# A decoder layer on one core: z_b projected before z_a, and silu(z_a) kept in SBUF instead of sent through DRAM

## The chip, the cores and the metric

The kernel runs on one core of a Trainium2 chip. The metric is device time in microseconds for one execution: the median of the timed runs. Five engines work side by side, each through its own instruction list in order: TensorE (PE in the rows; PEld is its weight load), VectorE (DVE), ScalarE (ACT), GpSimd (POOL) and SyncE (SP), which here only issues transfers. ACT and POOL issue some transfers too.

## The reference: what is computed

One inference step of a hybrid decoder layer, for 1024 prompt positions and 64 sample positions with the same weights (all float32).

```python
h = x @ w_in + b_in        # split into a_val, a_gate, z_a (1024 wide), q, k, v, z_b (512), g_a, g_b (1024)
u = a_val * sigmoid(a_gate)
conv_raw = depthwise_conv(u, width 31)
attn = combination of three groups of dilated window attention over q, k, v
c  = silu(layer_norm(conv_raw + conv_b, conv_ln_g, conv_ln_b))
pa = (c * silu(z_a)) @ w_a
pb = (attn * silu(z_b)) @ w_b
m  = sigmoid(g_a) * pa + sigmoid(g_b) * pb
y  = layer_norm(ALPHA * x + m @ w_out, ln_g, ln_b)
```

The convolution's layer norm runs over the 1024 channels of a position. The key/value buffers and the last 30 rows of `u` are outputs too.

## The kernel before, in words

Activations lie with 128 channels on the partitions and the 1088 positions along the row. The positions are cut into three chunks (`CHUNKS`: 384, 352 and 352). A tile of a projection is 128 output channels by 1088 positions. For precision every operand of a projection is kept as a rounded part and a remainder (`hi` and `lo`, `xhi` and `xlo`, `hbh` and `hbl`, `hah` and `hal`); `split` makes them, the rounded part by a copy on ACT (L100), the remainder by a subtraction on DVE (L101). Each chunk is then a run of matmuls (L171) with three products for each 128 input channels: 24 matmuls for 1024 input channels, 12 for the 512 of w_b.

A chunk gathers in one of three PSUM banks (`mm`), from which ACT or DVE moves it out. Weight tiles come through two buffers each of `raw`, `hi` and `lo` (`load_w`). Everything else lies in numbered slots of a row each (`slot(i, ...)`), and in small half-row tiles: `sb`, `P` and `PT`, two buffers each.

The stages that matter here come at the end:

- After attention, `gate` projects a tile of g_b, g_a or z_a, applies sigmoid or silu on ACT on the way out of PSUM (`gst`, L730), and sends the row to DRAM (`sgb`, `sga`, `sza`, L732). The eight tiles of g_b and the eight of g_a are done by then.
- The layer norm of the convolution: the eight rows `cv` are read back from DRAM, their mean over channels is a sum on DVE (`chan_mean`) and a matmul with `ones` (L773); then the mean is subtracted (L777), squared on ACT and summed (L783), a second matmul with `ones` (L790) gives the variance, and each row is scaled (L803) and goes through silu (L804). Meanwhile PE projects four tiles of z_a.
- Then the four tiles of z_b, each followed by one more tile of z_a. A chunk of z_b goes through silu (ACT, L818), is multiplied by `attn` (DVE, L819) and split into `hbh` and `hbl`, by way of the half-row tile `sb`.
- Stage w_b: eight tiles with the weights `w_b`, 12 matmuls a chunk. Each chunk leaves PSUM by a multiplication with its piece of sigmoid(g_b) into `tf` (L839), the piece having been loaded from `sgb` into `P` or `PT` by SP (`ld`, L829). In the same stage silu(z_a) is loaded back from `sza` into `sb`, chunk by chunk, multiplied by `cv` on DVE (L848) and split into `hah` and `hal`, which take the memory of `xhi` and `xlo` (named `x` in the rows).
- Stage w_a: eight tiles with the weights `w_a` on `hah` and `hal`; then the projection w_out and the last layer norm.

The program order below is not the order on the engines: a scheduler places each engine's instructions by its own model, at build time. On the chip each engine keeps that order and waits where something is not ready.

Of the kernel before, what the change touches and what calls it, by code (L numbers as in the profile page):

```python
# [8 lines left out]
F32 = mybir.dt.float32  # L9
F32R = mybir.dt.float32r  # L10
AF = mybir.ActivationFunctionType
ALU = mybir.AluOpType
# [4 lines left out]
P = 128  # L17
# [4 lines left out]
NT = NP_ + NS  # L22
CHUNKS = ((0, 384), (384, 352), (736, 352))
# [4 lines left out]
F_AVAL, F_AGATE, F_ZA, F_Q, F_K, F_V, F_ZB, F_GA, F_GB = 0, 8, 16, 24, 36, 48, 60, 64, 72  # L28
# [13 lines left out]
def trunk_kernel(ctx, tc, I, O):  # L42
    nc = tc.nc
    sync, act, dve, pool, pe = nc.sync, nc.scalar, nc.vector, nc.gpsimd, nc.tensor
# [8 lines left out]
    dram = ctx.enter_context(tc.tile_pool(name="dram", bufs=1, space=DRAM))  # L53
# [3 lines left out]
    def nm(s):  # L57
        uid[0] += 1
        return f"{s}_{uid[0]}"

    def slot(i, shape, dt=F32, n="s"):
        return sp.tile(shape, dt, tag=f"S{i}", name=nm(n))

    def xslot(i, shape, dt=F32R, n="x"):
        return xs.tile(shape, dt, tag=f"X{i}", name=nm(n))

    def half(tag, shape, bufs, dt=F32):
        return hp.tile(shape, dt, tag=tag, bufs=bufs, name=nm(tag))
# [30 lines left out]
    def split(dst_hi, dst_lo, src):  # L99
        h = act.activation(out=dst_hi, in_=src, func=AF.Copy)  # L100
        dve.tensor_tensor(out=dst_lo, in0=src, in1=dst_hi.bitcast(F32), op=ALU.subtract)  # L101
        return h
# [7 lines left out]
    def load_w(src, n, raw=None, parts=1):  # L110
        if raw is None:
            raw = wp.tile([P, D], F32, tag="raw", name=nm("raw"))
            sync.dma_start(out=raw[:, :n], in_=src)
        hi = wp.tile([P, D], F32R, tag="hi", name=nm("hi"))
        lo = wp.tile([P, D], F32R, tag="lo", name=nm("lo"))
        with tc.high_priority(HP):
            for i in range(0, n, n // parts):
                s = split(hi[:, i:i + n // parts], lo[:, i:i + n // parts], raw[:, i:i + n // parts])
            pace(s)
        return hi, lo  # L120
# [53 lines left out]
    def proj(parts, evac):  # L174
        for ci, (c0, cn) in enumerate(CHUNKS):
            evac(ci, c0, cn, proj_chunk(parts, c0, cn))

    def in_proj(f, evac, w=None):
        hi, lo = w or load_w(I["w_in"][f], D)
        proj([(hi, lo, xhi, xlo)], evac)  # L180
# [28 lines left out]
    def rotate(key, slots):  # L209
        i = rot.get(key, 0)  # L210
        rot[key] = i + 1
        return slots[i % len(slots)]
# [89 lines left out]
    def visit(burst=None):  # L302

        with tc.high_priority(700):
            gate = pipe[-1]["exp"] if pipe else None
            if pipe and "pts" not in pipe[-1]:
                transposes(pipe[-1])
            if len(pipe) == 2 or burst is None:
                values(pipe.pop(0), gate)
            if burst:  # L310
                scores(burst, gate)
                pipe.append(burst)

    def together(m, gate):
        tc.add_manual_dep(m.ins, gate.ins.name, SYNC, reason="the row starts complete")
# [249 lines left out]
    for u, (f, g) in enumerate(units):  # L565
# [16 lines left out]
        if u in B_CONV:  # L582
            c = B_CONV.index(u)
# [137 lines left out]

    sga = dram.tile([8, P, NT], F32, name="sga")
    sgb = dram.tile([8, P, NT], F32, name="sgb")
    sza = dram.tile([8, P, NT], F32, name="sza")

    def gate(f, func, dst):
        st = slot(rotate("gst", GST), [P, NT], n="gst")

        def ev(ci, c0, cn, ps):
            act.activation(out=st[:, c0:c0 + cn], in_=ps, func=func, bias=b_sb[:, f:f + 1])  # L730
        in_proj(f, ev)
        pool.dma_start(out=dst, in_=st)  # L732

    GST = [3, 4]
    gates = ([(F_GB + i, AF.Sigmoid, sgb[i]) for i in range(8)] + [(F_GA + i, AF.Sigmoid, sga[i]) for i in range(8)]
             + [(F_ZA + i, AF.Silu, sza[i]) for i in range(8)])
    credit[1] = 0.0
    for pr in range(4):
        sc = sample_scores(pr)
# [10 lines left out]
            gate(*gates.pop(0))  # L750
    sample_out()
    credit[1] = 1.25
    GST[:] = [4, 5]
    cv = []
    for c in range(8):
        t = slot(6 + c, [P, NT], n="cv")
# [30 lines left out]
    for c0, cn in CHUNKS:  # L787
        ps = o_ps()
        s = slice(c0, c0 + cn)
# [14 lines left out]
        act.activation(out=cv[c], in_=cv[c], func=AF.Silu, scale=clg[:, c:c + 1], bias=clb[:, c:c + 1])  # L804


    hb_slots = (18, 19, 20, 21, 22, 23, 2, 3)
    hbh, hbl = [], []
    for _ in range(4):
        gate(*gates.pop(0))  # L810
    for f in range(4):
        hh = slot(hb_slots[2 * f], [P, NT], F32R, n="hbh")
        hl = slot(hb_slots[2 * f + 1], [P, NT], F32R, n="hbl")

        def ev(ci, c0, cn, ps, f=f, hh=hh, hl=hl):
            s = slice(c0, c0 + cn)
            z = half("sb", [P, 384], 2)
            act.activation(out=z[:, :cn], in_=ps, func=AF.Silu, bias=b_sb[:, F_ZB + f:F_ZB + f + 1])  # L818
            dve.tensor_tensor(out=z[:, :cn], in0=z[:, :cn], in1=attn[f][:, s], op=ALU.mult)  # L819
            split(hh[:, s], hl[:, s], z[:, :cn])  # L820
        in_proj(F_ZB + f, ev)
        hbh.append(hh)
        hbl.append(hl)
        gate(*gates.pop(0))


    def ld(tag, src, c0, cn):
        t = half(tag, [P, 384], 2)
        sync.dma_start(out=t[:, :cn], in_=src[:, c0:c0 + cn])  # L829
        return t[:, :cn]  # L830

    tf = []
    for i in range(8):
        hi, lo = load_w(I["w_b"][i], 512)
        t = slot((0, 1, 14, 15, 16, 17, 4, 5)[i], [P, NT], n="tf")
        sg = [ld(rotate("sg", ("P", "PT")), sgb[i], c0, cn) for c0, cn in CHUNKS]

        def ev(ci, c0, cn, ps, t=t, sg=sg):
            dve.tensor_tensor(out=t[:, c0:c0 + cn], in0=ps, in1=sg[ci], op=ALU.mult)  # L839
        proj([(hi, lo, hbh, hbl)], ev)  # L840
        tf.append(t)
    hah, hal = [], []
    for c in range(8):
        hh, hl = xslot(c, [P, NT]), xslot(8 + c, [P, NT])
        for c0, cn in CHUNKS:
            s = slice(c0, c0 + cn)
            z = ld("sb", sza[c], c0, cn)
            dve.tensor_tensor(out=z, in0=z, in1=cv[c][:, s], op=ALU.mult)  # L848
            split(hh[:, s], hl[:, s], z)
        hah.append(hh)  # L850
        hal.append(hl)
    for i in range(8):
# [7 lines left out]


    woh, wol = [], []
    wo_slots = (18, 19, 20, 21, 22, 23, 2, 3, 6, 7, 8, 9, 10, 11, 12, 13)
    for k in range(8):
        raw = wp.tile([P, D], F32, tag="raw", name=nm("raw"))
        sync.dma_start(out=raw, in_=I["w_out"][:, k])
# [9 lines left out]
    while copies:  # L876
        dst, src = copies.pop(0)
        act.dma_start(out=dst, in_=src)
    for t in range(9):
        n = min(P, NT - t * P)  # L880
# [8 lines left out]
        for hf in range(2):  # L889
            ps = mm_ps()  # L890
            s = slice(512 * hf, 512 * hf + 512)
# [14 lines left out]
        for hf in range(2):  # L906
            s = slice(512 * hf, 512 * hf + 512)
# [138 lines left out]
```

## Time and profile before

| what | value |
|---|---|
| median of three timed runs | 1432.5 us (1430.51 to 1432.59) |
| the profiled execution, its own time | 1428.53 us |
| its span, first to last instruction | 1426.7 us |
| PE busy | 1400.8 us, 98% of the span |
| DVE busy | 843.2 us, 59% |
| ACT busy | 448.6 us, 31% |
| mean granted TensorE clock | 0.996 of full speed |

The profiled execution took 1.8 us more than its span, and was 4.0 us shorter than the median. Busy shares are averages over all stages. "Idle before" or "waited for" is the time that an engine stood still before an instruction, with what ended that wait.

### The profile page before, as it was taken

Reading aid. Unit: us, or ns where it says so; the run is one execution under the profiler, and the core shown is the slowest. Engines: PE = TensorE matmul, PEld = TensorE weight load, DVE = VectorE, ACT = ScalarE, POOL = GpSimd, SP = SyncE. Lnnn points to the kernel's source line nnn. Section 1 sums busy time; section 2 is a strip of 40 time slices with the busy share of each in tenths; the row PEclk is TensorE's granted clock in tenths of the full one; section 3 lists DMA queues with packets and bytes.
Section 4 is the critical chain, followed back from the end, with each engine's and each line's share of the span. In section 5 each row is a group of like instructions: output and inputs, shape, how many; then the busy total and the mean of one; then the engine's idle time right before and its main releaser. Section 6 shows DMA issues by size and latency. Waiting matters only on the chain.

```text
span 1426.7 us, 22026 instructions
## 1 busy us (share of the span) xinstructions
PE 1400.8 (98%) x8656; PEld 1266.4 (89%) x8656; DVE 843.2 (59%) x1642; ACT 448.6 (31%) x997; POOL 157.8 (11%) x310
## 2 busy tenths in 40 slices
PE   8999999999999999999999999999999998999997
PEld 8989888899999999999886798887999998999885
DVE  4223131329858789599899784852368235536676
ACT  5204041134434434255431222112247222203210
POOL 1010111110111101103342201000000000000000
PEclk9999999999999999999999999999999999999999
DMA  7629385366655775655579647658755467435321
GB/s 225 218 79 352 119 293 208 90 219 200 217 178 184 231 200 175 219 193 139 165 252 356 242 182 267 243 194 329 251 169 171 169 209 242 152 92 165 113 94 59
DMA packets 91590, 280.19 MB, mean 196 GB/s; under 512 B 21632, under 2 KB 47552, under 8 KB 90080
## 3 DMA queue, kind: packets, MB, share of 16 engines
q1 hardware_dynamic: 76032, 151.62, 32.0%
q10 hardware_dynamic: 2816, 87.30, 17.5%
q0 software_dynamic: 12640, 39.88, 8.5%
q8 instruction: 68, 1.11, 0.3%
q14 instruction: 34, 0.28, 0.1%
HBM read 240.85 MB, written 125.20 MB: 257 GB/s over the span
## 4 chain that ended last, share of the span: by engine, by line
PE 43%; DMA 5%; DVE 3%; issue 0%; SPq 0%; ACT 0%; DVEq 0%
PE mm L171 31%; PE mm L896 7%; DMA sb<-sza 3%; DMA kv<-in_g2k_dram 1%; PE O L685 1%; DMA cv<-cvd 1%; PE S L640 1%; DVE cv L514 1%; PE O L693 1%; PE S L648 1%; DVE x L101 1%; PE S L652 0%; PE O L699 0%; DMA kv<-in_g3v_dram 0%; DVE sb L848 0%
## 5 line engine op out<-in xcount | busy, mean ns | idle before, releaser
L171 PE MATMUL mm<-x,hi 128*128 128x352 f32 (+1 forms) x3648 | 916.6, 331 | 7.2 <-ACT x L100 7.2
L171 PEld LDWEIGHTS mm<-x,hi 128*128 128x128 f32 x3648 | 645.5, 189 | 42.1 <-issue 28.9
L171 PE MATMUL mm<-x,lo 128*128 128x352 f32 (+1 forms) x1824 | 601.1, 330 | 0.4 <-DVE lo L101 0.4
L171 PEld LDWEIGHTS mm<-x,lo 128*128 128x128 f32 x1824 | 343.7, 188 | 12.9 <-issue 10.8
L514 DVE SCALAR_TENSOR_TENSOR cv<-ub,conv_w,cv 128x1024 f32<-128x1024 f32 x240 | 306.6, 1278 | 1.9
L100 ACT ACTIVATE hi<-raw 128x1024 fp32r<-128x1024 f32 (+2 forms) x87 | 85.9, 988 | 236.6 <-PE mm L171 185.8
L101 DVE TENSOR_TENSOR lo<-raw,hi 128x1024 fp32r<-128x1024 f32 (+2 forms) x87 | 98.7, 1134 | 100.7 <-ACT hi L100 100.6
L269 PE MATMUL mm<-vhi,x 128*128 128x512 f32 x384 | 119.2, 390 | 0.0
L348 ACT ACTIVATE P<-P,st 128x128 f32<-128x128 f32 (+1 forms) x192 | 84.2, 441 | 70.1 <-DVE st L341 69.5
L730 ACT ACTIVATE gst<-mm,b_in 128x352 f32<-128x352 f32 (+1 forms) x72 | 40.2, 560 | 145.2 <-PE mm L171 103.7
L269 PEld LDWEIGHTS mm<-vhi,x 128*128 128x128 f32 x384 | 72.1, 188 | 15.0 <-issue 0.2
L270 DVE TENSOR_TENSOR vst<-mm,vb 128x512 f32<-128x512 f32 x24 | 16.6, 692 | 104.5 <-PE mm L269 104.5
L269 PE MATMUL mm<-vlo,x 128*128 128x512 f32 x192 | 74.9, 390 | 0.0
L516 DVE SCALAR_TENSOR_TENSOR cv<-keep,conv_w,cv 128x64 f32<-128x64 f32 x240 | 67.7, 282 | 3.3
L341 DVE CUSTOM_DVE_ANT_0 P<-S,bias 128x128 f32<-128x128 f32 (+1 forms) x192 | 54.9, 345 | 10.6 <-PE S L331 10.6
L896 PE MATMUL mm<-wol,mh 128*128 128x512 f32 (+1 forms) x144 | 56.1, 390 | 0.0
L896 PE MATMUL mm<-woh,mh 128*128 128x512 f32 (+1 forms) x144 | 56.1, 389 | 0.0
L896 PE MATMUL mm<-woh,ml 128*128 128x512 f32 (+1 forms) x144 | 56.0, 389 | 0.0
L631 POOL COPY qf<-keep 64x16 f32<-64x16 f32 x96 | 41.5, 444 | 29.5 <-PE S L640 14.6
L269 PEld LDWEIGHTS mm<-vlo,x 128*128 128x128 f32 x192 | 36.0, 188 | 7.5 <-issue 0.2
L368 DVE COPY PT<-PT 128x512 f32<-128x512 f32 x36 | 24.6, 684 | 27.4 <-PE PT L360 26.1
L100 ACT ACTIVATE vhi<-raw 128x1024 fp32r<-128x1024 f32 x12 | 12.7, 1060 | 87.9 <-PE mm L277 80.2
(183 smaller groups left out, 1317.1 us busy)
## 6 DMA issues: line engine op xcount, KB each, us to landing
out_nb_dram<-in_cache_dram ACTq DMA_DIRECT2D x64, 1020.0 KB
raw<-in_w_in_dram SPq DMA_DIRECT2D x67, 512.0 KB
kv<-in_g3k_dram SPq DMA_DIRECT2D x32, 512.0 KB
kv<-in_g3v_dram SPq DMA_DIRECT2D x32, 512.0 KB
out_nb_dram<-in_cache_dram ACTq DMA_DIRECT2D x16, 1008.0 KB
kv<-in_g2k_dram SPq DMA_DIRECT2D x16, 512.0 KB
kv<-in_g2v_dram SPq DMA_DIRECT2D x16, 512.0 KB
raw<-in_w_v_dram SPq DMA_DIRECT2D x12, 512.0 KB
```

The source lines that it names most:

```text
L100: h = act.activation(out=dst_hi, in_=src, func=AF.Copy)
L101: dve.tensor_tensor(out=dst_lo, in0=src, in1=dst_hi.bitcast(F32), op=ALU.subtract)
L171: pe.matmul(ps[:, :cn], a, b, start=(i == 0), stop=(i == len(ops) - 1))
L269: pe.matmul(ps, a, b, start=(i == 0), stop=(i == len(ops) - 1))
L341: dve.tensor_tensor_reduce(out=pr[:, h, c], in0=ps[:, h, c], in1=un["bias"][:, h, b0:b0 + nk], scale=-1.0, scalar=3e38, op0=ALU.add, op1=A ...
L348: x["exp"] = act.activation(out=pr[:, h, c], in_=pr[:, h, c], func=AF.Exp, scale=-1.0, bias=st[:, t, h, 0:1], accum_out=st[:, t, h, 1:2])
L368: dve.tensor_copy(out=dst, in_=src)
L514: dve.scalar_tensor_tensor(out=acc[:, :NP_], in0=ub[:, j:j + NP_], scalar=w, in1=acc[:, :NP_], op0=ALU.mult, op1=ALU.add)
L516: dve.scalar_tensor_tensor(out=accs, in0=us[:, :, j:j + 8], scalar=w, in1=accs, op0=ALU.mult, op1=ALU.add)
L631: pool.tensor_copy(out=qfull(g)[hs, f].rearrange("p (r j h) -> p r j h", r=4, j=4)[:, :, :, 2 * f + h2], in_=qs[hs, g * 4 + f, 16 * pr:16 ...
L730: act.activation(out=st[:, c0:c0 + cn], in_=ps, func=func, bias=b_sb[:, f:f + 1])
L896: pe.matmul(ps[:n], a, b, start=(i == 0), stop=(i == len(ops) - 1))
```

## The change

The four tiles of z_b are projected first, while the layer norm runs, and the eight tiles of z_a after them. silu(z_a) stays in one of four slots (4, 5, 16, 17) and is multiplied into `cv` in place, a whole row at a time, after `cv` has been through its own silu. The DRAM buffer `sza`, the eight stores to it, the 24 loads back and their 24 multiplications are gone. The split into `hah` and `hal` is now made on whole rows of 1088 instead of chunks. Some slots are numbered anew, since z_b's results are now made while slots 2 and 3 still hold the layer norm's sums.

```diff
-    sza = dram.tile([8, P, NT], F32, name="sza")
-
-    def gate(f, func, dst):
-        st = slot(rotate("gst", GST), [P, NT], n="gst")
+    def gated(f, func, i):
+        st = slot(i, [P, NT], n="gst")
 
         def ev(ci, c0, cn, ps):
             act.activation(out=st[:, c0:c0 + cn], in_=ps, func=func, bias=b_sb[:, f:f + 1])
         in_proj(f, ev)
-        pool.dma_start(out=dst, in_=st)
+        return st
+
+    def gate(f, dst):
+        pool.dma_start(out=dst, in_=gated(f, AF.Sigmoid, rotate("gst", (3, 4))))
...
-    hb_slots = (18, 19, 20, 21, 22, 23, 2, 3)
+    hb_slots = (18, 19, 20, 21, 22, 23, 14, 15)
     hbh, hbl = [], []
-    for _ in range(4):
-        gate(*gates.pop(0))
     for f in range(4):
...
         in_proj(F_ZB + f, ev)
         hbh.append(hh)
         hbl.append(hl)
-        gate(*gates.pop(0))
+
+    for c in range(8):
+        dve.tensor_tensor(out=cv[c], in0=cv[c], in1=gated(F_ZA + c, AF.Silu, (4, 5, 16, 17)[c % 4]), op=ALU.mult)
...
-        t = slot((0, 1, 14, 15, 16, 17, 4, 5)[i], [P, NT], n="tf")
+        t = slot((0, 1, 2, 3, 16, 17, 4, 5)[i], [P, NT], n="tf")
...
     for c in range(8):
         hh, hl = xslot(c, [P, NT]), xslot(8 + c, [P, NT])
-        for c0, cn in CHUNKS:
-            s = slice(c0, c0 + cn)
-            z = ld("sb", sza[c], c0, cn)
-            dve.tensor_tensor(out=z, in0=z, in1=cv[c][:, s], op=ALU.mult)
-            split(hh[:, s], hl[:, s], z)
+        split(hh, hl, cv[c])
         hah.append(hh)
         hal.append(hl)
```

Two places on the engines' lists. The first is ACT between the last input projection and stage w_b (`x` is here the memory of `hah`, `hi` the rounded weights of a w_b tile, `gst` the last tile of z_a). Before:

```order
L730 ACTIVATE gst_10165<-mm_10173,b_in_195 128x384
L730 ACTIVATE gst_10165<-mm_10199,b_in_195 128x352
L100 ACTIVATE x_10701<-sb_10703 128x384
L100 ACTIVATE x_10701<-sb_10708 128x352
L100 ACTIVATE hi_10310<-raw_10308 128x512
L137 DMA out_nb_dram<-in_cache_dram 16x7680 x2
L730 ACTIVATE gst_10165<-mm_10225,b_in_195 128x352
```

And now, at the same place:

```order
L729 ACTIVATE gst_10164<-mm_10198,b_in_195 128x352
L100 ACTIVATE x_10700<-cv_9053 128x1088
L100 ACTIVATE x_10704<-cv_9055 128x1088
L100 ACTIVATE x_10708<-cv_9057 128x1088
L100 ACTIVATE x_10712<-cv_9059 128x1088
L100 ACTIVATE x_10716<-cv_9061 128x1088
L100 ACTIVATE x_10720<-cv_9063 128x1088
L100 ACTIVATE x_10724<-cv_9065 128x1088
L100 ACTIVATE hi_10309<-raw_10307 128x512
L137 DMA out_nb_dram<-in_cache_dram 16x7680 x2
L729 ACTIVATE gst_10164<-mm_10224,b_in_195 128x352
```

Between the second and the third chunk of the last z_a tile there stood two half-row splits, and now seven splits of whole rows.

The second is DVE in the layer norm, from the subtraction of the mean on (`lo` is the remainder of a weight tile, `vtot` the sum of squares). Before:

```order
L777 TENSOR_TENSOR cv_9066<-cv_9066,mean_9078 128x1088
L777 TENSOR_TENSOR cv_9068<-cv_9068,mean_9078 128x1088
L101 TENSOR_TENSOR lo_9423<-raw_9420,hi_9422 128x1024
L783 TENSOR_TENSOR vtot_9088<-vtot_9088,sq_9092 128x1088
L783 TENSOR_TENSOR vtot_9088<-vtot_9088,sq_9096 128x1088
L783 TENSOR_TENSOR vtot_9088<-vtot_9088,sq_9100 128x1088
```

And now, with the chunks of z_b among them (the multiplications of `sb` and the remainders `hbl`):

```order
L776 TENSOR_TENSOR cv_9065<-cv_9065,mean_9077 128x1088
L776 TENSOR_TENSOR cv_9067<-cv_9067,mean_9077 128x1088
L101 TENSOR_TENSOR lo_9459<-raw_9456,hi_9458 128x1024
L816 TENSOR_TENSOR sb_9350<-sb_9350,attn_3784 128x352
L782 TENSOR_TENSOR vtot_9087<-vtot_9087,sq_9091 128x1088
L816 TENSOR_TENSOR sb_9389<-sb_9389,attn_5247 128x384
L101 TENSOR_TENSOR hbl_9256<-sb_9350,hbh_9255 128x352
L782 TENSOR_TENSOR vtot_9087<-vtot_9087,sq_9095 128x1088
```

The last chunk of the second z_b tile and the first of the third are worked off behind all eight subtractions of the mean.

## Rows read from the trace of the kernel before

**Rows 1.** The page, its first part: the span, and TensorE's busy time.

```profile
span 1426.7 us, 22026 instructions
PE 1400.8 (98%) x8656; PEld 1266.4 (89%) x8656; DVE 843.2 (59%) x1642; ACT 448.6 (31%) x997; POOL 157.8 (11%) x310
```

**Rows 2.** Stretches of the last third: length, then busy time (and instructions) of PE, PEld, DVE, ACT, POOL, then granted clock, DMA share and GB/s. They are the layer norm with z_a and z_b, stage w_b, the first two tiles of w_a, and the other six tiles of w_a.

```profile
1030.22:1164.53 134.31, 134.31 (x805) 132.92 (x806) 67.63 (x72) 63.67 (x87) 3.72 (x7) 1.00 0.53 172
1164.53:1220.37 55.84, 50.34 (x289) 48.82 (x289) 31.15 (x62) 13.37 (x25) 0.54 (x1) 0.97 0.76 246
1220.37:1248.57 28.20, 25.96 (x146) 25.07 (x146) 14.16 (x26) 5.05 (x8) 0.00 (x0) 0.94 0.44 140
1248.57:1319.89 71.32, 71.32 (x434) 71.32 (x434) 35.18 (x57) 15.35 (x22) 0.00 (x0) 1.00 0.42 128
```

**Rows 3.** What PE waited for from 1000 us to the end: total, times, longest.

```profile
PE mm L171 <- ACT x L100: 2.7, 2, 2.2
PE mm L171 <- DVE tf L839: 2.5, 2, 2.2
PE mm L171 <- ACT hi L100: 2.5, 1, 2.5
PE O L773 <- DVE tot L766: 0.5, 1, 0.5
```

**Rows 4.** Stage w_b tile by tile, from the first matmul of a tile to the first of the next: length, PE busy time, granted clock, DMA share, GB/s.

```profile
1164.53:1170.47 5.94, 5.94 (x37) 1.00 0.70 220
...
1182.98:1191.64 8.66, 6.42 (x36) 1.00 0.68 214
...
1198.27:1206.91 8.64, 6.18 (x38) 1.00 0.82 241
1206.91:1214.44 7.53, 7.53 (x36) 0.77 0.80 254
1214.44:1220.37 5.93, 5.93 (x38) 1.00 0.59 176
```

**Rows 5.** Waits of DVE, of ACT and of SP's queue from 1150 to 1235 us: total, times, longest.

```profile
DVE sb L848 <- DMA sb<-sza: 33.6, 20, 4.3
...
ACT x L100 <- DVE sb L848: 46.5, 20, 4.7
...
SPq L829 <- DVE x L101: 17.3, 12, 4.4
SPq L829 <- DVE tf L839: 13.2, 11, 3.3
```

**Rows 6.** PE's timeline after one of its waits: start, length, instruction, and in brackets the idle time before it with what ended it.

```profile
1206.91 0.54 PE L171 MATMUL mm<-hbh,hi 128*128 128x384 f32 x1 [2.46 <-ACT hi L100]
1207.24 0.52 PE L171 MATMUL mm<-hbl,hi 128*128 128x384 f32 x1
...
1210.62 0.32 PE L171 MATMUL mm<-hbh,hi 128*128 128x352 f32 x1
```

**Rows 7.** The transfers from and to `sgb`, from the view of that tensor: time from issue to landing.

```profile
DMA to landing us min/median/max: 2.9/4.1/8.4
```

**Rows 8.** Timeline of ACT at the end of the last z_a tile, with the transfers that its queue issues (ACTq), and of PE at the first matmul of the third chunk of stage w_b.

```profile
1160.91 0.56 ACT L730 ACTIVATE gst<-mm,b_in 128x352 f32<-128x352 f32 x1 [3.28 <-PE mm L171]
1161.40 0.91 ACT L100 ACTIVATE x<-sb 128x384 fp32r<-128x384 f32 x2
1164.57 0.63 ACT L100 ACTIVATE hi<-raw 128x512 fp32r<-128x512 f32 x1 [2.26 <-PE mm L171]
1164.57 1.16 ACTq L137 DMA_DIRECT2D out_nb_dram<-in_cache_dram  x2
1165.78 0.56 ACT L730 ACTIVATE gst<-mm,b_in 128x352 f32<-128x352 f32 x1 [0.58 <-issue]
...
1168.56 0.32 PE L171 MATMUL mm<-hbh,hi 128*128 128x352 f32 x1
```

**Rows 9.** Groups of instructions from 1017 to 1240 us, shapes kept apart: busy time, mean ns of one, idle time before them.

```profile
L803 DVE TENSOR_TENSOR cv<-cv,rstd 128x1088 f32<-128x1088 f32 x8 | 9.7, 1282 | 0.0
...
L101 DVE TENSOR_TENSOR lo<-raw,hi 128x512 fp32r<-128x512 f32 x8 | 5.5, 684 | 2.1 <-ACT hi L100 2.1
...
L839 DVE TENSOR_TENSOR tf<-mm,P 128x352 f32<-128x352 f32 x8 | 4.1, 516 | 1.4 <-PE mm L171 1.4
...
L100 ACT ACTIVATE hi<-raw 128x1024 fp32r<-128x1024 f32 x14 | 14.8, 1058 | 21.3 <-PE mm L171 21.3
...
L100 ACT ACTIVATE x<-sb 128x384 fp32r<-128x384 f32 x8 | 4.2, 524 | 15.1 <-DVE sb L848 15.1
```

**Rows 10.** Timeline of DVE and PE in the layer norm: the sum over channels, the matmul that waits for it, the eight subtractions of the mean, the next weight remainder, and the first matmuls of the first two chunks of PE's fourth tile (of z_a then).

```profile
1027.45 2.62 DVE L766 TENSOR_TENSOR tot<-tot,cv 128x1088 f32<-128x1088 f32 x2 [8.23 <-DMA cv<-cvd]
1030.22 0.88 PE L773 MATMUL O<-tot,ones 128*128 128x384 f32 x2 [0.46 <-DVE tot L766]
1041.46 9.71 DVE L777 TENSOR_TENSOR cv<-cv,mean 128x1088 f32<-128x1088 f32 x8 [9.51 <-ACT mean L774]
1051.09 1.22 DVE L101 TENSOR_TENSOR lo<-raw,hi 128x1024 fp32r<-128x1024 f32 x1
...
1055.81 0.51 PE L171 MATMUL mm<-x,hi 128*128 128x384 f32 x2
...
1059.99 0.48 PE L171 MATMUL mm<-x,hi 128*128 128x352 f32 x2
```

More of the change, by code (lines that the diff above doesn't have):

```diff
@@ L731, in gate @@
         in_proj(f, ev)
-        pool.dma_start(out=dst, in_=st)
-    GST = [3, 4]
-    gates = ([(F_GB + i, AF.Sigmoid, sgb[i]) for i in range(8)] + [(F_GA + i, AF.Sigmoid, sga[i]) for i in range(8)]
-             + [(F_ZA + i, AF.Silu, sza[i]) for i in range(8)])
+        return st
+    def gate(f, dst):
+        pool.dma_start(out=dst, in_=gated(f, AF.Sigmoid, rotate("gst", (3, 4))))
+    gates = [(F_GB + i, sgb[i]) for i in range(8)] + [(F_GA + i, sga[i]) for i in range(8)]
     credit[1] = 0.0
@@ L752, in trunk_kernel @@
     credit[1] = 1.25
-    GST[:] = [4, 5]
     cv = []
@@ L862, in trunk_kernel @@
     woh, wol = [], []
-    wo_slots = (18, 19, 20, 21, 22, 23, 2, 3, 6, 7, 8, 9, 10, 11, 12, 13)
+    wo_slots = (18, 19, 20, 21, 22, 23, 14, 15, 6, 7, 8, 9, 10, 11, 12, 13)
     for k in range(8):
```

## The prediction, made before the change was run

> **What bounds the kernel now.** I read the page's first part: PE is busy 1400.8 of 1426.7 us [rows 1]. So an idle stretch of DVE, ACT or a queue matters only where PE then stands, and all that a change of order can give back is PE's idle time and time at a lower clock. The stretches say where that is [rows 2]: in the layer norm with z_a and z_b, 1030.22 to 1164.53, PE is busy for the whole 134.31 us. In stage w_b it is busy 50.34 of 55.84 us, in the first two tiles of w_a 25.96 of 28.20, and in the next six it has no gap, 71.32 us, which is 11.89 a tile.
>
> What would these stages take undisturbed? The first and the last tile of w_b have no gap and full clock, 5.94 and 5.93 us [rows 4]. Eight such tiles are 47.5 us, eight of w_a 95.1, together 142.6. They took 55.84 + 28.20 + 71.32 = 155.4. **The excess is 12.7 us.** The list of PE's waits [rows 3] names 7.7 of it: for ACT `x` L100 2.7, DVE `tf` L839 2.5, ACT `hi` L100 2.5. The other 5.0 is PE busy but slower: 50.34 - 47.5 = 2.8 in w_b, 25.96 - 23.78 = 2.2 in the two tiles of w_a. The tile from 1206.91 shows how: no gap, granted clock 0.77, 7.53 us [rows 4], and ahead of it a gap of 2.46 us [rows 6], behind which matmuls start 0.33 us apart, twice the distance of a full-speed tile (5.94 us over 36 matmuls is 0.165). So at least that gap brought the lower of the two levels (1.2 instead of 2.4 GHz), and it goes with its gap.
>
> The waits of the other engines say what was late [rows 5]. DVE waited 33.6 us in 20 pieces for `sb<-sza`, transfers of silu(z_a); ACT's splits waited 46.5 us for those DVE results. `sb` has two buffers, and SP's queue, which issues these loads and those of `sgb` in one list (L829), waited 17.3 us for DVE to free `x`'s source and 13.2 for `tf`. Each list runs in order: behind a DVE that waits for `sza` stand the `tf` that empty PSUM and the `lo` of the weights; behind an ACT that waits for DVE stands `hi`. All three of PE's releasers are such instructions.
>
> **What goes.** The 24 loads, 24 multiplications and 24 half-row splits, with the waits for them. I count the whole excess as gone: **-12.7**. What could keep some of it is the loads of `sgb`, which remain (a rival below). The eight stores on POOL's queue go too; PE waits for none of them [rows 3]: 0.
>
> The layer norm's first `ones` matmul waited 0.46 us for `tot` [rows 3, 10], which is ready at about 1030. In the new order it stands 14 matmuls later on PE, 14 x 0.165 = 2.3 us, so this wait goes: **-0.5**.
>
> **What moves: z_b into the layer norm.** Twelve chunks put four short operations each there: ACT a silu (0.56, as rows 8 have for 352 columns) and a rounding (0.52 for 384), DVE two operations like `tf` (0.52) [rows 9]. That is 12 x 1.04 = 12.5 us for DVE in a stretch in which it is busy 67.6 of 134.3 [rows 2], and most of it was in this stretch before; what matters is the order around the long run of eight subtractions, 9.71 us, which waits for the mean [rows 10]. Two things can be late behind it. First `lo`, the weight remainder, which ended at 1052.3. One chunk's pieces more ahead of it put it at about 1053.3; PE wants it with the third matmul of its fourth tile, 1056.3 - 0.5 = 1055.8. Margin 2.5. Second the PSUM bank for the second chunk of that tile, wanted at 1060.0 - 0.4 = 1059.6. DVE starts the run near 1042.3 (one chunk's pieces behind 1041.46) and then has 9.7 + 1.2 + 0.5 + 1.2 + 0.5 + 0.5 = 13.6 of work until an `sb` is free, 1055.9; ACT has a weight rounding (1.06) and shorter work, some 2.2 in all, before the silu that empties the bank, which ends near 1058.6. Margin 1.0, an estimate. So I take 0, with bounds 0 and +3: a wait of 1.0 for a run that is 2 us late, and as much and half again at the lower clock.
>
> **What is added: whole-row splits at the seam.** On ACT seven whole-row splits now stand ahead of `hi` and of the third `gst`, where two half-row splits stood. In before ACT's first split there starts at 1161.40, and the two of 384 columns take 0.91 together [rows 8], though each lasts 0.52 [rows 9]: some 0.13 of each is overlap at 0.455 spacing. For 1088 columns I go from 1024 columns, 1.06 [rows 9], to 1.11, less overlap 0.09: 1.02 apart, an estimate. Seven end at 1161.4 + 7.1 = 1168.5. `hi` and its two DMA issues took 1.21 from start to the start of `gst` (1164.57 to 1165.78): `gst` then starts at 1169.75 and, with 0.56 of its own, frees its PSUM bank at 1170.3; PE's matmul follows at about 1170.45. That bank is one of three; PE wants it for the third chunk of the first w_b tile, at 1168.56 [rows 8]. **+1.9 us.** Bounds: 0, if the splits are 0.74 apart or closer, and 3.5, if the gap is followed by a lower clock as the one of 2.46 was (1.6 on the next tile). Next late is DVE: seven remainders of 1.21 (9.71 / 8), two `tf` and a `lo` (0.68) end near 1172.6; the second w_b tile wants that `lo` at about 1173.1, after the 1.9. It costs nothing more; but if ACT's splits alone were faster, that `lo` would be 1.4 late, and only 0.5 would be gained.
>
> The gap's mechanism has a rule speaking for it: the Trainium skill (Perfetto Trace Analysis, "Optimizing Scalar/DVE Operations") says that where Scalar and Vector aren't saturated but cause bubbles on other engines, breaking up instructions may let work end sooner. Here ACT is busy 13.37 of 55.84 us in stage w_b, and the change does the opposite, 24 splits to 8. By the rule in its strong form, chunks again, the sum would lose the 1.9 and be -13.2; by the rows it is with it.
>
> **Sum.** -12.7 - 0.5 + 1.9 = **-11.3**. The profiled execution's own time is 1428.5, so 1417.2 by it; the median of the timed runs lies 4.0 above that one. **1421.2 for the median, 1421.**
>
> **Rivals.**
> *All stalls gone, the seam too.* If splits run faster or `gst` slips earlier: 1432.5 - 13.2 = 1419.3. For it: ACT and DVE have much idle time. Against it: both work their lists in order, the seven splits stand there, and DVE's remainders would have to be faster as well.
>
> *The loads of `sgb` become the bound of w_b.* They stay, chunk by chunk in four half-row buffers, and took 2.9 to 8.4 us, median 4.1 [rows 7]. PE works a chunk off in 5.94 / 3 = 1.98, so four buffers go round in 7.9 us; a transfer may take about 6.9 with issue and `tf` (1.0). At the median nothing waits. If all took 8.4, a round would be 9.4, 1.5 too long, in six rounds 9.2 us: 1430.4. Half of that: 1426. For it: the DMA share is 0.59 to 0.82 in these tiles [rows 4], with weights beside it. Against it: the `sza` loads, as many chunks as `sgb` has, leave just that share.
>
> *The trip was hidden and nothing changes.* A rule would have it so: the Trainium skill (DMA: Bandwidth & Descriptors, "Rules for kernel authors") has the transfer issued early and waited for late, so that its fixed cost lies under the compute. The trace doesn't agree, DVE stood 33.6 us for these loads. But PE's own waits name DVE and ACT, never a DMA; if they came from the weights' transfers, the time would stay at 1432.5 - 0.5, 1432.
>
> *Slower: z_b's way out of PSUM behind the layer norm.* Place: fourth tile of PE, 1056 to 1064, behind the subtractions. It decides when it loses over 11.3 us more than I count, so when the bank comes 1.0 + 11.3 = 12.3 us later than worked out: DVE's 13.6 us run would have to double, or seven chunks lose 2 us each, 14 us, which gives 1435.2, 1436 with some low clock. For it: the first three tiles must all pass two `sb` buffers. Against it: PE had no idle time there with DVE half idle [rows 2].
>
> **How the numbers follow.** Forecast, 1421, with its own range 1419 to 1424 (up to 1422.8 with the clock's 1.6, and some of the +3): 0.64. Seam free, 1416 (by half of the scatter of the median's 4.0 over the profile) to 1419.3: 0.11. `sgb`, 1424 to 1430: 0.14. Hidden, 1430 to 1433: 0.06. Slower: 0.05. Range 1416 to 1427, which leaves out the last two and a third of the `sgb` case, some 0.15. What a measurement of this kernel can tell from no change is 0.2%, 2.9 us: faster is below 1429.6, slower above 1435.4. Faster: 0.64 + 0.11 + 0.12 = 0.87; same 0.09 (hidden, the upper end of `sgb`, the lower of slower); slower 0.04.
>
> **What would show it.** In the profile of the changed kernel: no waits of DVE for `sza`; PE's waits from 1000 us on reduced to one at the third chunk of the first w_b tile, of about 1.9 us, released by ACT `gst`; w_b tiles of 5.94 otherwise and granted clock 1.00 there; w_a in 95.1; no wait at the `ones` matmul. It is wrong if PE waits between 1040 and 1080 us for `lo`, `hbl` or a bank, if DVE's `tf` waits for `P` or `PT` from `sgb`, or if `x` L100 stays a releaser over more than one tile.

## The result: 0.67% faster, and the profile after

Timed by turns with the kernel before, the changed kernel took 1422.8 us, the kernel before 1432.2 (medians of 18 each). The ratio is 0.9933, with a 95% interval of 0.9917 to 0.9948: 9.6 us less, 7.4 to 11.9. The profiled execution took 1416.9 us, 11.6 less than that of before (1428.5).

First the page's first part and the stretches of the changed kernel. The columns are those of [rows 2]; the stretches are the layer norm from its first `ones` matmul on, stage w_b, and all eight tiles of w_a.

```profile
span 1415.2 us, 21885 instructions
PE 1396.6 (99%) x8656; PEld 1263.4 (89%) x8656; DVE 841.1 (59%) x1610; ACT 444.8 (31%) x981; POOL 156.3 (11%) x302
```
```profile
1032.38:1164.16 131.78, 131.78 (x791) 130.40 (x791) 72.42 (x72) 62.67 (x84) 0.00 (x0) 1.00 0.39 133
1164.16:1213.00 48.84, 47.63 (x288) 47.20 (x287) 26.66 (x39) 10.94 (x14) 0.00 (x0) 1.00 0.69 223
1213.00:1308.21 95.21, 95.21 (x581) 95.21 (x579) 43.05 (x69) 17.41 (x23) 0.00 (x0) 1.00 0.41 121
```

Stage w_b took 48.8 us instead of 55.8, and w_a is one gapless run of 95.2 at full clock. PE is busy 4.2 us less in total [rows 1], although it does the same matmuls. Some 3.4 us of that is the lower clock that is gone, an estimate: 7.53 us at 0.77 lose 1.7 [rows 4], and 28.20 us at 0.94 lose 1.7 [rows 2]. The rest is not the clock. Matmuls overlap (of 352 columns each lasts 0.32 us, and the next starts 0.16 behind it), so a wait also costs PE busy time at its two ends. In the profile of trip kept, below, PE is busy 145.09 us in stages w_b and w_a at a granted clock of 1.00; in that of first three splits only, where PE has no wait there, it is busy 142.67.

Next the waits from 1000 us on, by engine (PE), and from 1150 to 1235 for SP's queue. The columns are those of [rows 3, 5].

```profile
PE mm L171 <- DVE lo L101: 1.2, 1, 1.2
...
SPq L828 <- DVE tf L838: 42.0, 22, 13.4
SPq L113 <- DVE lo L101: 16.8, 11, 10.5
SPq L828 <- DVE tf L853: 15.8, 5, 3.5
```

Of the four kinds of wait in [rows 3] none is left. One new one came: 1.2 us for a weight remainder. SP's queue still waits for buffers, up to 13.4 us, but no longer for one that a half-finished row of silu(z_a) holds, and neither PE nor DVE waits for a transfer there.

The place of the new wait is the seam from z_a to w_b. ACT first, then DVE, then PE at the first matmul of the third chunk of the first w_b tile, at the first of the second tile, and at the one that waited:

```profile
1161.04 4.12 ACT L100 ACTIVATE x<-cv 128x1088 fp32r<-128x1088 f32 x4
1164.28 1.16 ACTq L137 DMA_DIRECT2D out_nb_dram<-in_cache_dram  x2
1165.06 3.10 ACT L100 ACTIVATE x<-cv 128x1088 fp32r<-128x1088 f32 x3
1168.06 0.62 ACT L100 ACTIVATE hi<-raw 128x512 fp32r<-128x512 f32 x1
1168.58 0.53 ACT L729 ACTIVATE gst<-mm,b_in 128x352 f32<-128x352 f32 x1
...
1162.18 4.90 DVE L101 TENSOR_TENSOR x<-cv,x 128x1088 fp32r<-128x1088 f32 x4 [7.28 <-ACT x L100]
1167.46 2.48 DVE L101 TENSOR_TENSOR x<-cv,x 128x1088 fp32r<-128x1088 f32 x2
1170.30 1.28 DVE L101 TENSOR_TENSOR x<-cv,x 128x1088 fp32r<-128x1088 f32 x1
1171.50 0.69 DVE L101 TENSOR_TENSOR lo<-raw,hi 128x512 fp32r<-128x512 f32 x1
...
1168.20 0.32 PE L171 MATMUL mm<-hbh,hi 128*128 128x352 f32 x1
1170.11 0.34 PE L171 MATMUL mm<-hbh,hi 128*128 128x384 f32 x1
1172.24 0.44 PE L171 MATMUL mm<-hbh,lo 128*128 128x384 f32 x1 [1.21 <-DVE lo L101]
```

The seven splits take 7.0 us on ACT (7.1 worked out). But the third chunk of w_b starts at 1168.20, before the last `gst` even begins (1168.58): it did not need that bank. What ends last is DVE, whose seven remainders stand ahead of `lo`.

### The profile page after: what moved, and what is told of

It reads as the page before. It is cut to its first block, busy times and chain, and to the rows that moved or that the text cites. A ratio compares the mean times of both kernels' runs of the same rounds, so it can differ in the third digit from the quotient of the medians.

```text
span 1415.2 us, 21885 instructions
## 1 busy us (share of the span) xinstructions
PE 1396.6 (99%) x8656; PEld 1263.4 (89%) x8656; DVE 841.1 (59%) x1610; ACT 444.8 (31%) x981; POOL 156.3 (11%) x302
## 4 chain that ended last, share of the span: by engine, by line
PE 44%; DVE 3%; DMA 2%; issue 1%; SPq 0%; POOL 0%; ACT 0%; DVEq 0%; POOLq 0%
PE mm L171 33%; PE mm L891 7%; DVE cv L514 1%; PE O L685 1%; DMA kv<-in_g3v_dram 1%; PE S L640 1%; DMA kv<-in_g2k_dram 1%; PE O L693 1%; PE O L699 0%; DMA stn<-scr 0%; PE S L648 0%; DVE x L101 0%; PE S L652 0%; SPq L624 0%; PE O L700 0%
## 5 line engine op out<-in xcount | busy, mean ns | idle before, releaser
L100 ACT ACTIVATE vhi<-raw 128x1024 fp32r<-128x1024 f32 x12 | 12.7, 1060 | 88.1 <-PE mm L277 80.2
```

## The experiments

Since the whole time of one execution scatters by 10 us and more (below), each experiment is read twice: by its ratio to the kernel before, measured in the same rounds, and by the length of stages w_b and w_a together, from the first matmul on `hbh` to the first of w_out. Undisturbed these take 142.6 us, as the prediction worked out. Here are the nine profiles, in the columns of [rows 2], in this order: before, changed, then the experiments' kernels: trip kept, trip early, deep chunks, first three splits only, splits in chunks, and second profiles of before and of changed.

```profile
1164.53:1319.72 155.19, 147.46 (x865) 145.04 (x865) 80.32 (x145) 33.71 (x54) 0.54 (x1) 0.98 0.55 173
```
```profile
1164.16:1308.21 144.05, 142.84 (x867) 142.41 (x865) 69.71 (x108) 28.35 (x37) 0.00 (x0) 1.00 0.50 156
```
```profile
1162.62:1314.33 151.71, 145.09 (x865) 142.21 (x865) 80.97 (x145) 33.60 (x54) 0.54 (x1) 1.00 0.56 178
```
```profile
1175.30:1320.10 144.80, 143.31 (x867) 142.36 (x865) 69.65 (x108) 28.23 (x37) 0.54 (x1) 1.00 0.51 163
```
```profile
1170.64:1315.08 144.44, 142.98 (x866) 142.43 (x865) 71.07 (x124) 29.96 (x49) 0.54 (x1) 1.00 0.52 163
```
```profile
1163.46:1306.14 142.68, 142.67 (x866) 142.41 (x865) 70.16 (x109) 28.36 (x37) 0.00 (x0) 1.00 0.50 158
```
```profile
1169.24:1313.22 143.98, 142.76 (x867) 142.46 (x865) 70.48 (x121) 29.73 (x49) 0.00 (x0) 1.00 0.50 156
```
```profile
1176.16:1330.01 153.85, 147.39 (x867) 145.43 (x866) 80.70 (x145) 33.64 (x54) 0.54 (x1) 0.98 0.55 175
```
```profile
1174.72:1318.76 144.04, 142.83 (x866) 142.40 (x865) 70.17 (x109) 28.34 (x37) 0.00 (x0) 1.00 0.51 156
```

They fall in two groups, 152 to 155 and 143 to 145 us.

**Trip kept.** Is it the order of z_b and z_a that pays, or the trip? The new order, with the trip through DRAM put back:

```diff
     for c in range(8):
-        dve.tensor_tensor(out=cv[c], in0=cv[c], in1=gated(F_ZA + c, AF.Silu, (4, 5, 16, 17)[c % 4]), op=ALU.mult)
+        pool.dma_start(out=sza[c], in_=gated(F_ZA + c, AF.Silu, (4, 5, 16, 17)[c % 4]))
...
-        split(hh, hl, cv[c])
+        for c0, cn in CHUNKS:
+            s = slice(c0, c0 + cn)
+            z = ld("sb", sza[c], c0, cn)
+            dve.tensor_tensor(out=z, in0=z, in1=cv[c][:, s], op=ALU.mult)
+            split(hh[:, s], hl[:, s], z)
```

> The new order (z_b first), but silu(z_a) goes through DRAM as before: stored row by row, loaded back chunk by chunk into the two half-row buffers, multiplied and split there. Theory (the loads back, late in three in-order lists, cost the 12.7 us): DVE waits some 33 us for these loads again, PE's waits for ACT x, ACT hi and DVE tf in stage w_b and the first tiles of w_a come back with the lower clock behind them, and only the 0.5 us at the ones matmul stays gained: 1428 in a profiled execution, ratio to the kernel before 0.9995, within 0.997 to 1.002. Rival (the order of z_b and z_a is what pays): like the changed kernel, 1417 profiled, ratio 0.993.

Measured: ratio 1.0001 (0.9973 to 1.0029), 12 runs. The waits of DVE, from 1150 to 1240 us, and of PE from 1017 us on:

```profile
DVE sb L848 <- DMA sb<-sza: 26.5, 18, 3.9
...
PE mm L171 <- DVE tf L839: 3.9, 5, 1.1
PE mm L171 <- ACT x L100: 1.8, 1, 1.8
PE mm L171 <- ACT hi L100: 0.6, 1, 0.6
```

The same three releasers are back, and the gain is gone: the order alone brings nothing that the timing can tell. The wait of the `ones` matmul stayed away, as expected. In this profile the excess was 9.1 us, not 12.6: the waits were shorter ones, and the granted clock was 1.00 in the stretch, so the lower clock that was expected behind them did not come. Whether the smaller excess belongs to the order or to this one execution is not shown.

**Trip early.** The opposite: the old order, the same bytes through DRAM, but each row loaded back whole into a free slot.

```diff
+    for c in range(8):
+        z = slot((14, 15, 16, 17)[c % 4], [P, NT], n="z")
+        sync.dma_start(out=z, in_=sza[c])
+        dve.tensor_tensor(out=cv[c], in0=cv[c], in1=z, op=ALU.mult)
...
-        for c0, cn in CHUNKS:
-            s = slice(c0, c0 + cn)
-            z = ld("sb", sza[c], c0, cn)
-            dve.tensor_tensor(out=z, in0=z, in1=cv[c][:, s], op=ALU.mult)
-            split(hh[:, s], hl[:, s], z)
+        split(hh, hl, cv[c])
```

> The old order (four z_a, then z_b and z_a by turns), with the trip through DRAM, but each row of silu(z_a) is loaded back as a whole into one of four free slots as soon as it is stored, and multiplied into cv in place; splits of whole rows as in the changed kernel. Same bytes to and from DRAM as before. Theory (late loads, not the trip, cost the time): nearly all of the gain without the change of order: PE's waits for x, tf and hi gone, about 1417.5 profiled (the ones matmul's 0.5 stays, a wait of 1 to 2 us at the start of stage w_b as in the changed kernel), ratio 0.993 to 0.995. Rival 1 (the order pays): ratio 1.000. Rival 2 (the traffic itself pays): the weights and sgb loads stay slow, ratio 0.998 to 1.000.

Measured: ratio 0.9928 (0.9900 to 0.9956), 6 runs: the changed kernel's gain, with the trip. The waits of DVE and PE in the same windows as above:

```profile
DVE cv L835 <- DMA z<-sza: 16.5, 4, 6.2
...
PE mm L171 <- DVE lo L101: 1.2, 1, 1.2
PE O L773 <- DVE tot L766: 0.5, 1, 0.5
PE mm L171 <- DVE tf L844: 0.3, 1, 0.3
```

DVE still waits 16.5 us for `sza`, but three of its four waits end before stage w_b begins at 1175.30, and PE waits for no consequence of them but perhaps 0.3. (Once, at 1196, a `tf` waited 1.2 us for a piece of `sgb`; PE did not wait behind it.) So neither the traffic nor the order was the cost. The 1.2 at the seam is there as in the changed kernel, and the 0.5 at the `ones` matmul as in the kernel before: the three terms of the sum come apart one by one.

**Deep chunks.** Trip early also made 24 pieces into 8. Here the pieces are as before, in the same four slots (the edit against trip early):

```diff
         z = slot((14, 15, 16, 17)[c % 4], [P, NT], n="z")
-        sync.dma_start(out=z, in_=sza[c])
-        dve.tensor_tensor(out=cv[c], in0=cv[c], in1=z, op=ALU.mult)
+        for c0, cn in CHUNKS:
+            s = slice(c0, c0 + cn)
+            sync.dma_start(out=z[:, s], in_=sza[c][:, s])
+            dve.tensor_tensor(out=cv[c][:, s], in0=cv[c][:, s], in1=z[:, s], op=ALU.mult)
...
-        split(hh, hl, cv[c])
+        for c0, cn in CHUNKS:
+            s = slice(c0, c0 + cn)
+            split(hh[:, s], hl[:, s], cv[c][:, s])
```

> The old order with the trip through DRAM in the same pieces as before, 24 loads, 24 multiplications and 24 splits, and of the kernel before only this changed: the loads go into four whole-row slots, so twelve pieces can be on their way, where the kernel before had two half-row buffers. Theory (two buffers make the loads late): stages w_b and w_a together 144 to 145 us as with whole-row pieces, ratio to the kernel before 0.992 to 0.995. Rival (the number of pieces on DVE, ACT and SP's queue costs the time): at least half of the excess stays, 149 us or more, ratio 0.997 or more.

Measured: ratio 0.9934 (0.9907 to 0.9961), 12 runs, 144.4 us for the two stages. The number of pieces is not the cost. Against what the expectation says, one more thing differs from the kernel before: the product goes into `cv`, ahead of stage w_b in program order, and the splits read it there, so a split no longer holds the loaded piece. Room to load early and a product made early come together in this kernel and in trip early; they were not tried apart.

**First three splits only.** At the seam of the changed kernel, the second w_b tile's weights go ahead of the last five splits:

```diff
         hi, lo = load_w(I["w_b"][i], 512)
+        if i == 1:
+            wb1 = last[0]
...
-        split(hh, hl, cv[c])
+        if c < 3:
+            split(hh, hl, cv[c])
+        else:
+            with tc.issue_after(wb1[0].ins):
+                act.activation(out=hh, in_=cv[c], func=AF.Copy)
+            with tc.issue_after(wb1[1].ins):
+                dve.tensor_tensor(out=hl, in0=cv[c], in1=hh.bitcast(F32), op=ALU.subtract)
```

(`last[0]` holds the two instructions of the latest split.)

> The changed kernel, with only three of the eight whole-row splits ahead of the rounding of the second w_b tile's weights on ACT, and its remainder on DVE ahead of the fourth subtraction; the other five splits stand behind. Theory (that remainder, behind seven subtractions of 1.29 us on DVE, made PE wait 1.21 us): no wait of PE between 1160 and 1180, profiled 1416.9 - 1.2 = 1415.7, ratio to the kernel before lower by 0.001 than that of the changed kernel, which timing can hardly tell. Rival (the wait moves to the third tile, behind five subtractions): a wait of about 1 us near 1176, profiled 1416.9.

Measured: ratio 0.9903 (0.9871 to 0.9936), 6 runs, median 1417.0 against 1431.1 of before in the same rounds. DVE's timeline:

```profile
1161.48 3.69 DVE L101 TENSOR_TENSOR x<-cv,x 128x1088 fp32r<-128x1088 f32 x3 [7.28 <-ACT x L100]
1165.09 0.68 DVE L101 TENSOR_TENSOR lo<-raw,hi 128x512 fp32r<-128x512 f32 x1
...
1174.23 0.68 DVE L101 TENSOR_TENSOR lo<-raw,hi 128x512 fp32r<-128x512 f32 x1
```

The second tile's `lo` is there by 1165.8, the third's by 1174.9, in time for its tile near 1175.3 (1163.46 + 2 x 5.94). PE has no wait left in the two stages, and their 142.68 us are the undisturbed 142.6 of the prediction. The stages are 1.37 us shorter than in the changed kernel; the timed difference (0.003 in the ratio) lies within the overlapping intervals, so that it is faster than the changed kernel too is shown by the stage, not by the timing. It clearly beats the kernel before.

**Splits in chunks.** The changed kernel with its splits chunk by chunk. The Trainium skill (Perfetto Trace Analysis, "Optimizing Scalar/DVE Operations") says that breaking up instructions may let work be completed sooner where Scalar or Vector is not saturated but causes bubbles on other engines. The edit:

```diff
-        split(hh, hl, cv[c])
+        for c0, cn in CHUNKS:
+            s = slice(c0, c0 + cn)
+            split(hh[:, s], hl[:, s], cv[c][:, s])
```

> The changed kernel, with the splits into hah and hal made chunk by chunk again (24 on ACT and 24 on DVE instead of 8 and 8). Theory (what stands ahead of the second tile's weights counts, and small pieces cost more in sum): 20 roundings ahead of hi take 6 x 1.30 + 0.9 = 8.7 us instead of 7.0, so hi ends at 1170.3 and the remainder lo about 0.9 later than in the changed kernel: PE's wait there grows from 1.2 to about 2.1 us, profiled 1417.8. Rival (smaller pieces let other work in between): no wait, profiled 1415.7.

Measured: ratio 0.9919 (0.9890 to 0.9947), 6 runs. PE's wait stayed at 1.22 us, neither 2.1 nor none. DVE's timeline, and PE's at the matmul that waited:

```profile
1166.67 5.45 DVE L101 TENSOR_TENSOR x<-cv,x 128x384 fp32r<-128x384 f32 x12 [6.68 <-ACT x L100]
...
1176.52 0.68 DVE L101 TENSOR_TENSOR lo<-raw,hi 128x512 fp32r<-128x512 f32 x1
...
1177.25 0.44 PE L171 MATMUL mm<-hbh,lo 128*128 128x384 f32 x1 [1.22 <-DVE lo L101]
```

Reckoned from the start of stage w_b, DVE's first remainder starts at -2.57 us, with whole rows at -1.98: small pieces begin sooner, by 0.6. But from there to `lo` it is 9.85 us instead of 9.32: more pieces cost 0.5. The two cancel, so here the rule's gain did not come. My expectation counted only the cost, and on the wrong engine: ACT's `hi` did end 0.9 later (5.4 us into the stage instead of 4.5), but `lo` did not wait for it, because DVE was at its remainders and two `tf` without a gap until 1176.5.

**Second profiles** of both kernels, unchanged:

> The kernel before, unchanged, for a second profile of it. Theory (the 12.7 us over the undisturbed 142.6 are waits for loads that land later or sooner from one execution to the next): stages w_b and w_a together take 150 to 157 us, the excess between 8 and 14, with the same releasers. Rival (the excess is set by the order of the lists alone): 155.2 again within 0.5.

> The changed kernel, unchanged, for a second profile of it. Theory: stages w_b and w_a together take 144.0 us within 0.3 again, with the one wait of 1.2 us for the remainder of the second tile, whatever the whole execution takes; where it is longer than 1419 us, the difference lies in the sample attention between 600 and 800 us, as a wait of PE for POOL's copies (qf). Rival: a longer execution has its waits in the changed stages.

Measured: one execution each, 1438.8 and 1427.5 us, 10 longer than the first profiles. The two stages took 153.85 (before 155.19) and 144.04 (changed 144.05): what the kernel before loses there varies, 11.2 to 12.6 in the two executions (that its loads make it vary, as expected, is not shown); what the changed kernel takes is the same to 0.01. The 10 us lie elsewhere: in the changed kernel's second profile the first `ones` matmul stands at 1042.94 instead of 1032.38.

```profile
1032.38 0.81 PE L772 MATMUL O<-tot,ones 128*128 128x384 f32 x2
```
```profile
1042.94 0.81 PE L772 MATMUL O<-tot,ones 128*128 128x384 f32 x2
```

My expectation put them in the sample attention, as a wait for POOL's `qf`. That was wrong in size: of that wait only 1.4 us are there, and half of the 10.6 us is lost before the sample attention starts. PE's waits in this profile before 600 us (first row) and from 600 to 800 us:

```profile
PE PT L360 <- ACT P L348: 3.9, 2, 3.2
...
PE S L640 <- DMA kv<-in_g3k_dram: 2.3, 1, 2.3
PE S L648 <- POOL qf L631: 1.4, 2, 0.8
PE O L685 <- DMA kv<-in_g3v_dram: 1.3, 1, 1.3
```

## Why the prediction was right, step by step

- **The excess, -12.7.** Measured on the two profiles: 155.19 - 144.05 = 11.1 for the stages, with the new wait in it. Without that wait they take 142.68 (first three splits only), so 12.5 of the old excess went, all of it, and the new wait costs 1.4. The cause is shown by three kernels: with the late loads it stays (trip kept); with early loads, and the product made early with them, it goes though the bytes and the pieces stay (trip early, deep chunks). One reading in the term was too simple: the 5.0 of "PE busy but slower" is only some 3.4 of lower clock, the rest comes with the waits themselves, as said under the result.
- **The `ones` matmul, -0.5.** Right: no wait in the changed kernel, nor in trip kept, and 0.4 to 0.6 in every profiled kernel with the old order.
- **z_b in the layer norm, 0.** Right, with margins close to those worked out. DVE's run of subtractions, the `lo` behind it and the remainder that frees an `sb`, ACT's silu that empties the bank, and PE where it wants the first and the second, in the changed kernel:

```profile
1042.56 9.71 DVE L776 TENSOR_TENSOR cv<-cv,mean 128x1088 f32<-128x1088 f32 x8 [0.88 <-ACT mean L773]
1052.18 1.22 DVE L101 TENSOR_TENSOR lo<-raw,hi 128x1024 fp32r<-128x1024 f32 x1
1055.42 0.52 DVE L101 TENSOR_TENSOR hbl<-sb,hbh 128x352 fp32r<-128x352 f32 x1
...
1057.88 0.54 ACT L815 ACTIVATE sb<-mm,b_in 128x352 f32<-128x352 f32 x1
...
1055.82 0.35 PE L171 MATMUL mm<-x,lo 128*128 128x384 f32 x1
1059.65 0.48 PE L171 MATMUL mm<-x,hi 128*128 128x352 f32 x2
```

  `lo` ended at 1053.4 (1053.3 worked out) and was wanted at 1055.8: margin 2.4. The bank was empty at 1058.4 (1058.6) and wanted at 1059.65: margin 1.2 (1.0). The kernel has no more than that between it and a loss here.
- **The seam, +1.9.** The size was of the right order, a wait of 1.21 that costs 1.4, but the step that names the place failed. I had PE wait for ACT's last `gst` at the third chunk of the first w_b tile. Two errors made it: that chunk took another bank, for it began before `gst` did; and I took 1.21 from the start of `hi` to that of `gst` from [rows 8], where ACT's two transfer issues lie between them and ACT had nothing else queued. Here ACT issued them at 1164.28, beneath the splits, and `gst` came 0.52 behind the start of `hi`, at 1168.58 instead of 1169.75. What did wait is what the prediction named as next: `lo` 1.4 late, if ACT's part cost nothing. It was 1.2, and the clock stayed at 1.00 behind it. The overlap in the working is also misread (two splits of 0.52 that take 0.91 together stand 0.39 apart, not 0.455), but the spacing that came of it, 1.02, is near the 1.00 measured.
- **The remaining loads of `sgb`.** Not a bound: DVE's `tf` waited for PE and for no transfer there. (The rival's six rounds of 1.5 us are 9.0, not 9.2, and the times in [rows 7] take in the eight stores.)
- **The sum.** -12.7 - 0.5 + 1.9 = -11.3, so 1417.2 for the profiled execution, which took 1416.9. The two small errors offset each other: 0.5 too much at the seam against 0.2 too much of excess. That the sum meets this execution to 0.3 is in part luck, since two executions of one kernel differ by 10 us; the timed gain of 9.6 is 1.7 less than forecast, and 11.3 lies within its interval. The median is 1.6 above the 1421.2, because it lies 5.9 over its profiled execution and not 4.0: the first profile caught the shortest of 18 executions.

## What to carry to other kernels

An instruction that waits for a late load in an in-order list charges everything behind it: here 33.6 us of DVE's waiting for `sza` cost PE 12.5 us, in part through `tf` and `hi`, which needed none of that data. Before taking such a trip away, ask whether it can be made early: four whole-row buffers, with the loads and the product begun ahead of the stage, gave the gain that the timing can tell and kept the trip. And where a stage change hands an idle engine a batch of work, look for the small piece behind the batch that the next stage needs first, on each engine that takes part, and move that piece ahead.

## What the runs showed of the hardware

Transfers issued from ACT's own list cost ACT no time when it had work queued (two issues, 1.16 us together, beneath a gapless run of seven splits), and 0.58 us before the next instruction where it had not [rows 8].

The length of a wait did not decide alone whether the lower clock followed. In the kernel before, none came behind a wait of 2.18 us (granted clock 1.00 in 1191.64 to 1198.27), and in trip kept none behind 1.81 (1.00 in 1230.21 to 1234). In the second profile of the kernel before it came behind waits of 2.08 (0.70 in 1217.44 to 1221) and 1.69 (0.76 in 1244.28 to 1248).

The two profiles of the same program differ by some 10 us, and the difference arises ahead of the layer norm (its first `ones` matmul stands 11.6 us later in the second profile of the kernel before, 10.6 in that of the changed one); stages w_b and w_a differ by 1.3 us in the kernel before and by 0.01 in the changed one. In the profile of trip early, PE waited 5.6 us for POOL's `qf` copies. These came at 0.68 us each in a run of 18, with DVE busy 11.84 of the 12.22 us. In the changed kernel's profile the same run took 0.24 each, with DVE busy 1.99 of 4.40 us (708.00 to 712.40), but the eight copies behind it 0.73 each, with DVE busy for the whole 5.90 us (713.80 to 719.70). Over all 96 copies the two profiles have nearly the same mean, 469 and 459 ns. So the copies were slow in both profiles while DVE was busy, and PE waited where the slow ones came first; that DVE is the cause was not tried. The rows are POOL's copies in trip early and in the changed kernel.

```profile
711.24 12.22 POOL L631 COPY qf<-keep 64x16 f32<-64x16 f32 x18
```
```profile
708.09 4.31 POOL L631 COPY qf<-keep 64x16 f32<-64x16 f32 x18
713.80 5.83 POOL L631 COPY qf<-keep 64x16 f32<-64x16 f32 x8 [1.40 <-PE S L648]
```
